# A modulation's weights moved in the load queue, its second half summed in two bursts, and high parts of rows used first, in a two-layer Hyena and attention block

## The chip, the core and the metric

The kernel runs on one core of a Trainium2 chip. A core has TensorE (PE, matrix products), VectorE (DVE), ScalarE (ACT), GpSimd (POOL) and SyncE (SP, which here issues loads and stores). Each engine runs its own instructions in order and waits on semaphores for the others. The metric is the device time of one execution in microseconds. TensorE's clock is granted at one of two levels, 1.2 and 2.4 GHz; the profile shows which.

## The reference

A block of two layers works on 512 latent tokens and 256 context tokens of width 1024, all in float32. What matters here is the start of layer 0, a Hyena layer:

```
sh, sc, gt = split(silu(c) @ ada_w[0] + ada_b[0], 3)        # modulation, for c and for c_ctx
h  = rms_norm(x, norm_g[0]) * (1 + sc) + sh                  # 512 latent and 256 context rows
proj = h @ w_in                                              # 1024 -> 4 * 2048
filter: h = sin(freq * (z @ w1 + b1)); sin(.. w2 ..); sin(.. w3 ..); h @ w4, times a decay
x0, x1, v = short convolutions of proj;  u = x1 * v
y = (circular convolution of u with the filter + u * d) * x0 * silu(z),  then @ w_out
```

Layer 1 is attention with grouped heads; the change does not touch it.

## The kernel before

A float32 product is made from three matmuls on rounded parts: an operand is split into a high part (a cast to a 32-bit format with fewer bits) and a low part (the operand minus its high part), and high times high, high times low and low times high are added in PSUM. So every weight tile and every row of h needs a cast and a subtraction. Rows here are the eight blocks of 128 channels of h (k = 0 to 7); each has 512 latent and 256 context columns: `h_hi`, `h_lo` and `hc_hi`, `hc_lo`.

The program is written in one order per engine by hand: up to the first u (L685) every instruction of an engine follows the one written before it (the class `Engine`, L58, whose call is L69, so that nearly all rows of the first 70 us carry line L69). Behind that a scheduler orders the work.

How the start runs:

- SP loads x and the context (12 halves), then the weights of the modulation's shift and scale. These stand in two halves of the output channels, each as eight tiles of 512 KB (`ada0_load(dh, k)`, L344; tiles 2 to 7 of the first half as two loads). Between them stand the first two weight tiles of the projection (`st16`, `st32`: the tiles for x1 and v, L426) and the filter's last weights (`w4s0`). Eight loads are in flight at most: each waits for the one eight places ahead.
- TensorE multiplies the modulation's tiles as they come (`ada0`, L372, into `prow`); ScalarE copies the sums (`srow`), eight small matmuls turn them into columns (`padc`), and VectorE adds the bias and makes `ada` and `gsc` (`ada0_cols`, L380). The first half serves rows 0 to 3, the second rows 4 to 7.
- `load_w` (L125) splits a weight tile: the cast on ScalarE, the subtraction on GpSimd. `first_w` holds the tiles of the two outputs 16 and 32 (the second called `fw`) and of 17.
- `begin` (L595) interleaves rows and projections. `write(k)` calls `h_write` (L229): ScalarE scales and shifts (`raw` for rows 0 to 3, `hf` for 4 to 7), VectorE casts and subtracts, GpSimd subtracts for the context. `step(e, k)` is six matmuls of output e with row k (`in_step`, L580, into `pl` and `pc`).
- The third layer of the filter's small network (`mlp_mm(2)`, L283, then `mlp_arg`, a range reduction on VectorE, `mlp_sin`, `mlp_end` into `h3`) and the first group of the filter (`kfilter`, L475: `w4h`, `w4l`, then six `lags`, each two matmuls `pk` and a product `kfl` or `kfc`) are written among these.
- After `begin`, GpSimd issues four loads (kmat, kfwd) and starts `kdft` (L527): sums and differences `F0m`, their cast on ScalarE (`Fh0m`) and the low part (`Fl0m`), and so on, for the filter's transform; TensorE goes on with projections and later with the transform of u (`pu`).

The changed places are `h_write`, `mlp_end`, `ada0_cols`, the loads at L422 to L433, the first weights at L463 to L470, and `begin`.

Of the kernel before, what the change touches and what calls it, by code (L numbers as in the profile page):

```python
# [52 lines left out]
def hybrid_kernel(ctx: ExitStack, tc: tile.TileContext, x, ctxt, cols, fws, ada_w, hy_w_in, fw4, hy_w_out, at_w_in, at_q_g, at_k_g, at_w_out,  # L53
# [38 lines left out]
    def f(ap):  # L92
        return ap.bitcast(F32)
# [85 lines left out]
    def axt(name):  # L179
        return pa.tile([P, 512], F32, tag="ax", name=name, bufs=4)  # L180
# [48 lines left out]
    def h_write(k, src):  # L229

        t = raw.get(k)
        if t is None:
            t = cvtile(f"hf{k}")
        for s, hi, lo, c_, en in ((0, h_hi, h_lo, slice(0, LL), V), (1, hc_hi, hc_lo, slice(LL, T), G)):
            S.activation(t[:, c_], src(s), AF.Identity, bias=col_sh(0, s, k), scale=col_gsc(0, s, k))
            V.tensor_copy(hi[:, k, :], t[:, c_])
            r = en.tensor_tensor(lo[:, k, :], t[:, c_], f(hi[:, k, :]), ALU.subtract)
        hc_done.append(r)

# [14 lines left out]
    def cvtile(name):  # L254
        return hp.tile([P, T], F32, tag="cv", name=name, bufs=5)
# [58 lines left out]
    def mlp_sin(hh=0):  # L314
        aa = feat[0][:, hh * 384:hh * 384 + 384]
        S.activation(aa, aa, AF.Sin)

    def mlp_end():
        a = feat[0]
        if "h3" in dbg:  # L320
            SY.dma_start(dbg["h3"], a)
        h3t = hp.tile([P, T], F32R, tag="sz", name="h3t")
        V.tensor_copy(h3t, a)
        V.tensor_copy(h3[0:64], f(h3t[0:64]))
        V.tensor_tensor(h3[64:128], a[64:128], f(h3t[64:128]), ALU.subtract)
# [18 lines left out]
    def ada0_load(dh, k):  # L344

        c_ = slice(dh * 512, dh * 512 + 512)
        src = ada_w[0][k * P:(k + 1) * P, 0:2 * DM].rearrange("p (x o) -> p x o", x=2)[:, :, c_]
        two = "p (x o) -> p x o"
        if dh == 0 and k < 2:
            t = abtile(f"ad{dh}_{k}").rearrange(two, x=2)  # L350
        elif dh and k < 2:
            if k == 0:
                ad_st["big"] = kg.tile([P, 4, 512], F32, tag="kfl", name=f"ad{dh}_{k}")
            t = ad_st["big"][:, k * 2:k * 2 + 2, :]
        elif dh and k == 2:
# [24 lines left out]
    def ada0_cols(dh):  # L380
        srow = cvtile(f"srow{dh}")
        S.copy(srow[:, 0:512], prow[dh])
        padc = axt(f"padc{dh}")
        for j in range(4):
            TE.matmul(padc[:, j * 4:j * 4 + 4], srow[:, j * P:(j + 1) * P], sel2.rearrange("p x s -> p (x s)"),
                      start=True, stop=True)
        pv = padc[:, 0:16].rearrange("p (j x s) -> p s x j", x=2, s=2)
# [33 lines left out]

    for i in range(12):  # L422
        load_x(i)
    for k in range(6):
        ada0_load(0, k)
    st16, st32 = (wp.tile([P, 1024], F32, tag="stg", name=f"stg{e}", bufs=NST) for e in (16, 32))  # L426
    SY.dma_start(st16.rearrange("p (k e) -> p k e", k=KD), load_first(16))
    ada0_load(0, 6)
    SY.dma_start(st32.rearrange("p (k e) -> p k e", k=KD), load_first(32))
    ada0_load(0, 7)  # L430
    w4s0 = load_w4(0)
    for k in range(KD):
        ada0_load(1, k)  # L433
# [28 lines left out]
            ada0(0, 4 + k // 2)  # L462
    for i in range(1, 12, 2):  # L463
        scale_x(i, i in (3, 7, 11))
    first_w = {16: load_w(None, (KD, P), st=st16)}
    first_w[32] = load_w(None, (KD, P), st=st32, more=lambda i: [
        hp.tile([P, 1024], F32R, tag="AB", name=f"fw{x}", bufs=NAB) for x in range(2)])
    ada0(0, 6)
    ada0(0, 7)
    ada0_cols(0)  # L470


    kfs, kts = {}, {}
# [121 lines left out]
    def begin(es):  # L595

        for e in es:
            begun[e] = mmt(f"pl_{e}"), mmt(f"pc_{e}")
        pts = {}

        def write(k):
            h_write(k, (lambda s: raw[k][:, 0:LL] if s == 0 else raw[k][:, LL:T]) if k in raw else
                    (lambda s: pts[k][s][:, 0:LL if s == 0 else LC]))

        def step(e, k):
            cur[0] = in_step(first_w[e], *begun[e], k)
# [17 lines left out]
        first_w[17] = load_w(load_first(17), (KD, P))
        step(es[1], 3)
        ada0(1, 6)
        ada0(1, 7)
        ada0_cols(1)
# [880 lines left out]
```

## Time and profile before

| | us |
|---|---|
| median of 3 runs | 1477.99 (1475.77 to 1478.94) |
| profiled execution | 1477.03 |
| its span, first to last instruction | 1475.3 |
| TensorE busy in the span | 1433.8 (97%) |
| VectorE, ScalarE, GpSimd busy | 1081.9, 558.6, 488.5 |
| mean granted clock of TensorE | 0.994 of 2.4 GHz |

TensorE is busy 97% of the span, but its first slices are not full: in the page's row of 40 slices (36.9 us each) PE stands at 5 in the first and at 9 after it. GpSimd is busy a third of the whole, but 8.5 and 8.9 of 10 us in 70 to 80 and 80 to 90 us. Busy shares are averages over stages: here the reader has to look at who waits for whom in the first 110 us. A timeline row gives start, duration, engine, line, operation, output and inputs, count, and in brackets the idle time before it and what ended it. A chain row gives start, duration and what the end hung on. A DVE or POOL row that is longer than others of its shape holds a wait that is not shown as idle time.

### The profile page before, as it was taken

To read this page: it belongs to the slowest core of one execution; us is meant where nothing else is said; L and a number is where in the kernel's file an instruction comes from. 1 tells how busy PE (TensorE), PEld (TensorE's weight loads), DVE (VectorE), ACT (ScalarE), POOL (GpSimd) and SP (SyncE) were. 2 spreads that over 40 slices of the span, in tenths; PEclk is the share of its full clock that TensorE was granted. 3 is DMA by queue.
4 is the path that set the end of the run, shared out by engine and by line. 5 is a ranking of instruction groups with operands and counts; after the bars stand their busy time and mean duration, and the time that the engine had idled before them with its cause. 6 is when DMAs were issued, how large, how long until landed. Compare 5 with 4: busy or idle time off the path is not lost.

```text
span 1475.3 us, 23743 instructions
## 1 busy us (share of the span) xinstructions
PE 1433.8 (97%) x9271; PEld 1252.5 (85%) x9271; DVE 1081.9 (73%) x1904; ACT 558.6 (38%) x1089; POOL 488.5 (33%) x437
## 2 busy tenths in 40 slices
PE   5999999999999999999998999999999999999998
PEld 1688888888888888888887888799998998998987
DVE  3869769588695885968858354756886878878886
ACT  5332322323223233232333243634455444444442
POOL 1472735527345264462554451211100000000005
PEclk9999999999999999999999999999999999999999
DMA  9611433324223233232313774255222212212111
GB/s 321 187 52 57 122 87 90 93 76 122 80 82 111 72 115 93 79 108 79 90 55 109 275 274 159 75 166 170 91 90 86 86 44 78 94 44 72 58 61 69
DMA packets 177308, 157.58 MB, mean 107 GB/s; under 512 B 6771, under 2 KB 154891, under 8 KB 176684
## 3 DMA queue, kind: packets, MB, share of 16 engines
q1 hardware_dynamic: 173340, 135.10, 30.0%
q0 software_dynamic: 3712, 20.45, 4.0%
q8 instruction: 73, 1.20, 0.3%
q10 hardware_dynamic: 144, 0.52, 0.1%
q14 instruction: 39, 0.32, 0.1%
HBM read 138.20 MB, written 17.84 MB: 106 GB/s over the span
## 4 chain that ended last, share of the span: by engine, by line
PE 74%; DVE 16%; DMA 4%; POOL 3%; issue 1%; ACT 1%; SPq 1%; POOLq 0%; ACTq 0%; DVEq 0%
PE po L89 3%; PE po L90 3%; PE et L1293 3%; PE po L88 3%; PE pq L771 3%; DVE Y L724 3%; PE plx L582 3%; PE plx L583 2%; PE plx L586 2%; PE px L89 2%; PE px L88 2%; PE px L90 2%; PE pz L88 2%; PE pz L89 2%; PE pz L90 2%; PE pq L88 2%
## 5 line engine op out<-in xcount | busy, mean ns | idle before, releaser
L141 POOL TENSOR_TENSOR wlo<-stg,whi 128x1024 fp32r<-128x1024 f32 x63 | 154.1, 2446 | 202.2 <-ACT whi L140 201.4
L140 ACT CAST whi<-stg 128x1024 fp32r<-128x1024 f32 x97 | 101.8, 1050 | 251.1 <-issue 180.2
L1052 POOL TENSOR_TENSOR r2q<-s2q,mhalf 128x2 f32<-128x2 f32 x32 | 23.5, 733 | 342.1 <-DVE s2q L1050 342.1
L1281 ACT ACTIVATE E<-sc,st 128x768 f32<-128x768 f32 x64 | 57.7, 901 | 128.0 <-DVE st L1279 115.3
L582 PE MATMUL plx<-h_hi,whi 128*128 128x512 f32 x248 | 100.7, 406 | 0.0
L583 PE MATMUL plx<-h_lo,whi 128*128 128x512 f32 x248 | 98.1, 396 | 0.0
L586 PE MATMUL plx<-h_hi,wlo 128*128 128x512 f32 x248 | 98.1, 395 | 0.0
L1278 DVE TENSOR_REDUCE st<-sc 128x1 f32<-128x768 f32 x64 | 61.0, 953 | 16.6 <-PE sc L90 16.3
L585 PE MATMUL pcx<-hc_lo,whi 128*128 128x256 f32 x248 | 69.9, 282 | 0.0
L587 PE MATMUL pcx<-hc_hi,wlo 128*128 128x256 f32 x248 | 69.4, 280 | 0.0
L584 PE MATMUL pcx<-hc_hi,whi 128*128 128x256 f32 x248 | 69.4, 280 | 0.0
L1298 DVE TENSOR_TENSOR ptl<-et,pth 128x768 fp32r<-128x768 f32 x64 | 61.0, 954 | 5.3 <-ACT pth L1297 4.1
L931 DVE TENSOR_TENSOR yl<-yf,yh 128x768 fp32r<-128x768 f32 x26 | 25.8, 995 | 51.4 <-ACT yh L930 51.2
L1297 ACT CAST pth<-et 128x768 fp32r<-128x768 f32 x64 | 51.1, 799 | 31.1 <-PE et L1293 31.0
L585 PEld LDWEIGHTS pcx<-hc_lo,whi 128*128 128x128 f32 x248 | 46.7, 188 | 11.1
L584 PEld LDWEIGHTS pcx<-hc_hi,whi 128*128 128x128 f32 x248 | 46.7, 188 | 11.1
L90 PE MATMUL po<-pth,kvt 128*128 128x256 f32 x192 | 54.2, 283 | 0.0
L582 PEld LDWEIGHTS plx<-h_hi,whi 128*128 128x128 f32 x248 | 46.8, 189 | 8.7 <-issue 0.4
L89 PE MATMUL po<-ptl,kvt 128*128 128x256 f32 x192 | 54.1, 282 | 0.0
L88 PE MATMUL po<-pth,kvt 128*128 128x256 f32 x192 | 54.0, 281 | 0.0
L698 DVE TENSOR_TENSOR utl<-ut,uth 128x512 fp32r<-128x512 f32 (+1 forms) x32 | 16.4, 552 | 49.7 <-ACT uth L697 49.7
L1293 PE MATMUL et<-ident,E 128*128 128x128 f32 x384 | 52.3, 272 | 0.1
(911 smaller groups left out, 5129.0 us busy)
## 6 DMA issues: line engine op xcount, KB each, us to landing
stg<-in_hy_w_in_dram SPq DMA_DIRECT2D x64, 512.0 KB, 4.2
stg<-in_at_w_in_dram SPq DMA_DIRECT2D x40, 512.0 KB, 4.2
adw<-in_ada_w_dram SPq DMA_DIRECT2D x32, 512.0 KB, 3.8
yf<-y_scr POOLq DMA_DIRECT2D x32, 384.0 KB, 5.1
stg<-in_hy_w_out_dram SPq DMA_DIRECT2D x16, 512.0 KB, 5.5
stg<-in_at_w_out_dram SPq DMA_DIRECT2D x16, 512.0 KB, 3.6
dec<-in_k_dec_dram SPq DMA_DIRECT2D x48, 128.0 KB, 2.5
y_scr<-y SPq DMA_DIRECT2D x16, 384.0 KB, 3.2
```

The lines of the kernel that those rows point to most:

```text
L88: TE.matmul(ps, lh, rh, start=first, stop=False)
L89: TE.matmul(ps, lh, rl, start=False, stop=False)
L90: TE.matmul(ps, ll, rh, start=False, stop=last)
L140: S.copy(hi, st)
L141: (lo_eng or lo_default[0] or G).tensor_tensor(lo, st, f(hi), ALU.subtract)
L582: TE.matmul(pl, hi[:, k, :], h_hi[:, k, :], start=fi, stop=False)
L583: TE.matmul(pl, hi[:, k, :], h_lo[:, k, :], start=False, stop=False)
L584: TE.matmul(pc[:, 0:LC], hi[:, k, :], hc_hi[:, k, :], start=fi, stop=False)
L585: TE.matmul(pc[:, 0:LC], hi[:, k, :], hc_lo[:, k, :], start=False, stop=False)
L586: TE.matmul(pl, lo[:, k, :], h_hi[:, k, :], start=False, stop=la)
L587: return TE.matmul(pc[:, 0:LC], lo[:, k, :], hc_hi[:, k, :], start=False, stop=la)
L1293: TE.transpose(tp_[:, b * P:(b + 1) * P], E[:, b * P:(b + 1) * P], ident)
```

## The change

- The queue: all eight tiles of the modulation's first half are loaded ahead of `st16` and `st32`, which stood behind tiles 5 and 6.
- The first half's sums are copied and turned ahead of the split of the first weight tile. For output 32 the cast goes from ScalarE to VectorE (written behind the columns) and the subtraction on GpSimd behind row 0's.
- The second half's eight tiles are used in two bursts of four: after row 2, and while the range reduction runs. They were used in four pairs of two among rows 1 to 3. Copy and turn are separate functions now, `ada0_sum` and `ada0_turn`.
- In `h_write` both high parts of a row are made before the low parts; in `step` the six matmuls go in the order high by high, low weights by high rows, high weights by low rows.
- The third layer's matmuls and the filter's w4 split move from row 1 to row 2. Its `h3` is made by two copies on ScalarE and a subtraction on GpSimd, where VectorE did all three.
- Weight tile 17 is loaded and split ahead of the range reduction (it stood behind it), and each of the six lags stands a place later.

```
         t = raw.get(k)
...
+        parts = (h_hi, h_lo, slice(0, LL), V), (hc_hi, hc_lo, slice(LL, T), G)
+        for s, (hi, lo, c_, en) in enumerate(parts):
             S.activation(t[:, c_], src(s), AF.Identity, bias=col_sh(0, s, k), scale=col_gsc(0, s, k))
             V.tensor_copy(hi[:, k, :], t[:, c_])
+        for hi, lo, c_, en in parts:
             r = en.tensor_tensor(lo[:, k, :], t[:, c_], f(hi[:, k, :]), ALU.subtract)
...
-        V.tensor_copy(h3t, a)
-        V.tensor_copy(h3[0:64], f(h3t[0:64]))
-        V.tensor_tensor(h3[64:128], a[64:128], f(h3t[64:128]), ALU.subtract)
+        S.copy(h3t, a)
+        S.copy(h3[0:64], f(h3t[0:64]))
+        G.tensor_tensor(h3[64:128], a[64:128], f(h3t[64:128]), ALU.subtract)
...
+    def ada0_sum(dh):
+        srow[dh] = cvtile(f"srow{dh}")
+        S.copy(srow[dh][:, 0:512], prow[dh])
+
+    def ada0_turn(dh):
+        padc = padc_[dh] = axt(f"padc{dh}")
...
-    for k in range(6):
+    for k in range(KD):
         ada0_load(0, k)
...
-    ada0_load(0, 6)
     SY.dma_start(st32.rearrange("p (k e) -> p k e", k=KD), load_first(32))
-    ada0_load(0, 7)
...
-    first_w = {16: load_w(None, (KD, P), st=st16)}
-    first_w[32] = load_w(None, (KD, P), st=st32, more=lambda i: [
...
     ada0(0, 6)
     ada0(0, 7)
+    ada0_sum(0)
+    ada0_turn(0)
+    first_w = {16: load_w(None, (KD, P), st=st16)}
     ada0_cols(0)
+    fw32 = [hp.tile([P, 1024], F32R, tag="AB", name=f"fw{x}", bufs=NAB) for x in range(2)]
+    first_w[32] = [t.rearrange("p (a b) -> p a b", a=KD) for t in fw32]
+    V.tensor_copy(fw32[0], st32)
...
         def step(e, k):
-            cur[0] = in_step(first_w[e], *begun[e], k)
+
+            (hi, lo), (pl, pc), fi, la = first_w[e], begun[e], k == 0, k == KD - 1
+            for i, (w, l, c) in enumerate(((hi, h_hi, hc_hi), (lo, h_hi, hc_hi), (hi, h_lo, hc_lo))):
...
             write(i)
+            if i == 0:
+                G.tensor_tensor(fw32[1], st32, f(fw32[0]), ALU.subtract)
             step(es[0], i)
             if i:
                 step(es[1], i - 1)
-
-                ada0(1, 2 * i - 2)
-                ada0(1, 2 * i - 1)
-            if i == 1:
+            if i == 2:
+
+                for k in range(4):
+                    ada0(1, k)
                 mlp_mm(2)
                 lags += kfilter(0, w4s0)
-        for hh in range(2):
-            mlp_arg(2, hh)
-            mlp_sin(hh)
+        first_w[17] = load_w(load_first(17), (KD, P))
+        mlp_arg(2, 0)
+        mlp_sin(0)
+        for k in range(4, 8):
+            ada0(1, k)
+        ada0_sum(1)
+        mlp_arg(2, 1)
+        step(es[1], 3)
+        ada0_turn(1)
+        ada0_cols(1)
+        mlp_sin(1)
         mlp_end()
```

What this does to the order is shown at three places. First SP's queue, behind tile 5 of the modulation's first half (`ad`; `stg` are the projection's first two weight tiles, `hy_w_in`):

```order
-L69 DMA stg_159<-in_hy_w_in_dram 128x8x128
-L69 DMA ad_6_0_162<-in_ada_w_dram 128x512
-L69 DMA ad_6_1_163<-in_ada_w_dram 128x512
-L69 DMA stg_160<-in_hy_w_in_dram 128x8x128
-L69 DMA ad_7_0_167<-in_ada_w_dram 128x512
-L69 DMA ad_7_1_168<-in_ada_w_dram 128x512
+L69 DMA ad_6_0_159<-in_ada_w_dram 128x512
+L69 DMA ad_6_1_160<-in_ada_w_dram 128x512
+L69 DMA ad_7_0_163<-in_ada_w_dram 128x512
+L69 DMA ad_7_1_164<-in_ada_w_dram 128x512
+L69 DMA stg_167<-in_hy_w_in_dram 128x8x128
+L69 DMA stg_168<-in_hy_w_in_dram 128x8x128
```

Tiles 6 and 7 moved ahead of both weight tiles. Second, GpSimd from its first weight tile on, before:

```order
L69 TENSOR_TENSOR wlo_309<-stg_159,whi_308 128x1024
L69 TENSOR_TENSOR fw_313<-stg_160,fw_312 128x1024
L69 TENSOR_TENSOR hc_lo<-raw_254,hc_hi 128x256
L69 TENSOR_TENSOR hc_lo<-raw_265,hc_hi 128x256
L69 TENSOR_TENSOR w4l_376<-w4s_171,w4h_375 128x512
L69 TENSOR_TENSOR hc_lo<-raw_278,hc_hi 128x256
L69 TENSOR_TENSOR hc_lo<-raw_289,hc_hi 128x256
L69 TENSOR_TENSOR wlo_449<-stg_447,whi_448 128x1024
```

Four long pieces (128x512 and more) stand among the context's low parts. And now:

```order
L69 TENSOR_TENSOR wlo_320<-stg_167,whi_319 128x1024
L69 TENSOR_TENSOR hc_lo<-raw_254,hc_hi 128x256
L69 TENSOR_TENSOR fw_328<-stg_168,fw_327 128x1024
L69 TENSOR_TENSOR hc_lo<-raw_265,hc_hi 128x256
L69 TENSOR_TENSOR hc_lo<-raw_278,hc_hi 128x256
L69 TENSOR_TENSOR w4l_398<-w4s_171,w4h_397 128x512
L69 TENSOR_TENSOR hc_lo<-raw_289,hc_hi 128x256
L69 TENSOR_TENSOR wlo_423<-stg_421,whi_422 128x1024
L69 TENSOR_TENSOR h_116<-ma_396,h3t 64x768
```

The low part of fw stands between rows 0 and 1, w4l a row later, and the subtraction for h3 (`h`) is new on this engine. VectorE has the cast of fw (`fw_327`) between the columns and row 0. Third, ScalarE behind row 3, before (`ma` is the argument of the filter's last sine, `whi_448` weight tile 17):

```order
L69 ACTIVATE raw_289<-raw_289,ada_83,gsc_85 128x256
L69 ACTIVATE ma_374<-ma_374 128x384 x2
L69 CAST whi_448<-stg_447 128x1024
L69 COPY srow_463<-prow_365 128x512
L69 ACTIVATE hf_490<-xT_0_474,ada_83,gsc_85 128x512
```

Both sines stand ahead of the weight tile's cast. And now:

```order
L69 ACTIVATE raw_289<-raw_289,ada_83,gsc_85 128x256
L69 CAST whi_422<-stg_421 128x1024
L69 ACTIVATE ma_396<-ma_396 128x384
L69 COPY srow_444<-prow_383 128x512
L69 ACTIVATE ma_396<-ma_396 128x384
L69 CAST h3t<-ma_396 128x768
L69 CAST h_116<-h3t 64x768
L69 ACTIVATE hf_490<-xT_0_474,ada_83,gsc_85 128x512
```

The cast of weight tile 17 moved ahead of the sines, and the two copies for h3 came from VectorE.

## Rows read from the trace of the kernel before

**Rows 1.** Chain of waits, 13 to 38 us: start us, duration us, what.

```profile
20.44 2.45 SPq L69
...
22.93 6.79 DMA ad<-in_ada_w_dram
...
34.26 0.18 DVE ada L69
...
35.56 0.44 DVE h_hi L69
```

**Rows 2.** Timeline of TensorE, 24 to 55 us.

```profile
24.67 2.13 PE L69 MATMUL prow<-ad,silp 128*32 128x512 f32 x8
28.29 1.05 PE L69 MATMUL prow<-ad,silp 128*32 128x512 f32 x2 [1.49 <-DMA ad<-in_ada_w_dram]
29.77 1.90 PE L69 MATMUL prow<-ad,silp 128*32 128x512 f32 x2 [0.43 <-DMA ad<-in_ada_w_dram]
...
53.24 1.05 PE L69 MATMUL padc<-sel,srow 128*128 128x4 f32 x8 [0.84 <-ACT srow L69]
```

**Rows 3.** Windows: busy us (instructions) by engine, granted clock, DMA share, GB/s.

```profile
26.00:28.00 2.00, 0.80 (x3) 0.00 (x0) 0.39 (x1) 2.00 (x4) 0.00 (x1) 1.00 1.11 339
28.00:30.00 2.00, 1.28 (x3) 0.31 (x4) 0.00 (x0) 0.87 (x1) 2.00 (x1) 0.95 1.10 217
40.00:42.00 2.00, 2.00 (x14) 1.41 (x17) 1.97 (x4) 0.13 (x1) 1.76 (x2) 0.99 1.15 325
56.00:58.00 2.00, 1.38 (x5) 0.68 (x5) 1.28 (x5) 1.94 (x4) 0.00 (x0) 1.00 0.84 240
108.00:112.00 4.00, 3.66 (x15) 3.37 (x16) 1.84 (x3) 0.60 (x2) 1.82 (x1) 0.57 0.15 39
```

**Rows 4.** Chain of waits, 38 to 70 us.

```profile
43.61 0.67 DVE ma L69
...
50.82 0.53 ACT ma L69
...
56.06 0.79 ACT hf L69
```

**Rows 5.** Timeline of GpSimd, 69 to 75 us.

```profile
69.30 0.78 POOL L544 TENSOR_TENSOR F0m<-kfl 128x256 f32<-128x256 f32 x1
...
73.70 1.30 POOL L551 TENSOR_TENSOR Fl0m<-F0m,Fh0m 128x512 fp32r<-128x512 f32 x1 [0.58 <-ACT Fh0m L550]
```

**Rows 6.** Timeline of TensorE, 104 to 109 us.

```profile
107.61 0.38 PE L88 MATMUL pu<-uth,kfwd 128*128 128x256 f32 x1 [1.77 <-ACT uth L697]
```

**Rows 7.** Timeline of GpSimd, 28 to 55 us.

```profile
28.00 2.35 POOL L69 TENSOR_TENSOR wlo<-stg,whi 128x1024 fp32r<-128x1024 f32 x1 [9.23 <-ACT whi L69]
...
39.49 1.73 POOL L69 TENSOR_TENSOR w4l<-w4s,w4h 128x512 fp32r<-128x512 f32 x1
...
43.13 0.73 POOL L69 TENSOR_TENSOR hc_lo<-raw,hc_hi 128x256 fp32r<-128x256 f32 x1 [0.83 <-DVE hc_hi L69]
52.36 2.37 POOL L69 TENSOR_TENSOR wlo<-stg,whi 128x1024 fp32r<-128x1024 f32 x1 [8.49 <-ACT whi L69]
```

**Rows 8.** Timeline of VectorE, 36 to 56 us.

```profile
36.63 0.28 DVE L69 CAST hc_hi<-raw 128x256 fp32r<-128x256 f32 x1
...
40.00 1.38 DVE L69 CAST hc_hi<-raw 128x256 fp32r<-128x256 f32 x1
...
51.38 0.56 DVE L69 CAST h3t<-ma 128x768 fp32r<-128x768 f32 x1 [0.59 <-ACT ma L69]
...
52.54 3.01 DVE L69 TENSOR_TENSOR h<-ma,h3t 64x768 fp32r<-64x768 f32 x1
```

**Rows 9.** Timeline of ScalarE, 67 to 74 us.

```profile
67.50 1.05 ACT L140 CAST whi<-stg 128x1024 fp32r<-128x1024 f32 x1 [2.22 <-PE pc L69]
...
73.01 0.61 ACT L550 CAST Fh0m<-F0m 128x512 fp32r<-128x512 f32 x1
```

**Rows 10.** Waits, 0 to 80 us: who for whom, us in total, times, longest.

```profile
PE pc L69 <- POOL hc_lo L69: 0.8, 2, 0.4
```

More of the change, by code (lines that the diff above doesn't have):

```diff
@@ L233, in h_write @@
             t = cvtile(f"hf{k}")
-        for s, hi, lo, c_, en in ((0, h_hi, h_lo, slice(0, LL), V), (1, hc_hi, hc_lo, slice(LL, T), G)):
+        parts = (h_hi, h_lo, slice(0, LL), V), (hc_hi, hc_lo, slice(LL, T), G)
+        for s, (hi, lo, c_, en) in enumerate(parts):
             S.activation(t[:, c_], src(s), AF.Identity, bias=col_sh(0, s, k), scale=col_gsc(0, s, k))
             V.tensor_copy(hi[:, k, :], t[:, c_])
+        for hi, lo, c_, en in parts:
             r = en.tensor_tensor(lo[:, k, :], t[:, c_], f(hi[:, k, :]), ALU.subtract)
@@ L378, in ada0 @@
             TE.matmul(prow[dh][q:q + 32, :], silp[:, 2 * k:2 * k + 32], t, start=k < 2, stop=k >= KD - 2)
-    def ada0_cols(dh):
[L381 to L387, printed above, removed]
+    srow, padc_ = {}, {}
+    def ada0_sum(dh):
[3 more added lines that the diff above has]
+        padc = padc_[dh] = axt(f"padc{dh}")
+        for j in range(4):
+            TE.matmul(padc[:, j * 4:j * 4 + 4], srow[dh][:, j * P:(j + 1) * P], sel2.rearrange("p x s -> p (x s)"),
+                      start=True, stop=True)
+    def ada0_cols(dh):
+        pv = padc_[dh][:, 0:16].rearrange("p (j x s) -> p s x j", x=2, s=2)
         bv = vb[:, 32:48].rearrange("p (x k) -> p x k", x=2)[:, :, dh * 4:dh * 4 + 4]
@@ L464, in hybrid_kernel @@
         scale_x(i, i in (3, 7, 11))
-    first_w = {16: load_w(None, (KD, P), st=st16)}
-    first_w[32] = load_w(None, (KD, P), st=st32, more=lambda i: [
-        hp.tile([P, 1024], F32R, tag="AB", name=f"fw{x}", bufs=NAB) for x in range(2)])
     ada0(0, 6)
     ada0(0, 7)
+    ada0_sum(0)
+    ada0_turn(0)
+    first_w = {16: load_w(None, (KD, P), st=st16)}
     ada0_cols(0)
+    fw32 = [hp.tile([P, 1024], F32R, tag="AB", name=f"fw{x}", bufs=NAB) for x in range(2)]
+    first_w[32] = [t.rearrange("p (a b) -> p a b", a=KD) for t in fw32]
+    V.tensor_copy(fw32[0], st32)
     kfs, kts = {}, {}
@@ L605, in step @@
         def step(e, k):
-            cur[0] = in_step(first_w[e], *begun[e], k)
+            (hi, lo), (pl, pc), fi, la = first_w[e], begun[e], k == 0, k == KD - 1
+            for i, (w, l, c) in enumerate(((hi, h_hi, hc_hi), (lo, h_hi, hc_hi), (hi, h_lo, hc_lo))):
+                TE.matmul(pl, w[:, k, :], l[:, k, :], start=fi and i == 0, stop=la and i == 2)
+                cur[0] = TE.matmul(pc[:, 0:LC], w[:, k, :], c[:, k, :], start=fi and i == 0, stop=la and i == 2)
         lags = []
@@ L613, in begin @@
                 step(es[1], i - 1)
-                ada0(1, 2 * i - 2)
-                ada0(1, 2 * i - 1)
-            if i == 1:
+            if i == 2:
+                for k in range(4):
+                    ada0(1, k)
                 mlp_mm(2)
                 lags += kfilter(0, w4s0)
-        for hh in range(2):
-            mlp_arg(2, hh)
-            mlp_sin(hh)
-        mlp_end()
[L624 to L628, printed above, removed]
+        first_w[17] = load_w(load_first(17), (KD, P))
[9 more added lines that the diff above has]
+        mlp_sin(1)
+        mlp_end()
         for k in (4, 5):
@@ L632, in begin @@
             write(k)
-            lags.pop(0)()
+            if k > 4:
+                lags.pop(0)()
             if k in (5, 6):
@@ L638, in begin @@
                 step(es[1], 4)
-        for _ in range(2):
+        for _ in range(3):
             lags.pop(0)()
```

## The prediction

> **What bounds the kernel now.** The page first: the span is 1475.3 us and the profiled execution took 1477.03, so 1.7 us lie around the span, and it is 0.96 us below the median of the runs shown (1477.99). I make the sum on this execution and carry the difference to the median. Everything that the change moves stands before 74 us; behind that each engine runs the same instructions in the same order, so the question is by how much one hand-over point moves. I read the chain of waits over the first 70 us, then each engine's timeline there, then the windows for the granted clock, then the place near 106 us where TensorE waits again.
>
> In the chain the reader is to see a queue: the last tile of the modulation's first half lands at 29.72 (22.93 + 6.79), and the scale and shift columns (ada) are written at 34.26 [rows 1]. TensorE uses the tiles that it has until 26.8, waits 1.49 and 0.43 us for the last two and sums these at half clock [rows 2]: the granted clock is 0.95 in 28 to 30 and 0.99 in 40 to 42, so it fell to 1.2 of 2.4 GHz at 29.9 and rose at 40.0 [rows 3]. Then rows 0 to 3 are converted, VectorE does the range reduction of the filter's last sine until 50.8, and ScalarE begins rows 4 to 7 at 56.06 [rows 4]. The hand-over point is GpSimd's F0m at 69.30 [rows 5]: from there GpSimd works with few pauses until TensorE's pu, which waits 1.77 us and starts at 107.61 [rows 6]. So GpSimd's chain decides what a gain before 69.30 is worth, and it hands it on whole.
>
> **The change part by part.**
>
> *Queue.* Tiles 6 and 7 no longer stand behind 1.05 MB of projection weights. At the 339 GB/s of that stretch [rows 3] this is 3.1 us; and one issue that took 2.45 us [rows 1] was held up in the same queue. So the last tile lands at 26.6, or at 25.2 if half of that issue is won too. TensorE takes 2.13 us for the pairs of two tiles from 24.67 [rows 2], about 0.5 us a tile if none is missing; the sums are ready at 26.7 to 27.6 instead of 31.67. I take 26.7, since the tiles come faster than they are used. ScalarE copies the sums (0.6, at 27.6 with what stands ahead of it), eight small matmuls take 1.05 at full clock [rows 2]: ada at 28.7 instead of 34.26. If these 5.6 us stayed, the kernel would be 5 us faster. What is late next?
>
> *Weights after the turn.* ScalarE casts whi at 27.6 to 28.6 and GpSimd makes wlo at 28.6 to 30.9 (2.35, [rows 7]). Both stood under the wait for the modulation's weights, which covered them; now they stand beside the columns. (Weight tile 16 lands 1.6 us behind the last tile, 26.8 to 28.2: at the late end all of this moves by 0.6.) The high part of the second weight tile, fw, moves from ScalarE to VectorE, ahead of all row conversions. It could start at 29.3, after four small operations, and there GpSimd's wlo is running. What happens then the trace shows: the cast hc_hi takes 0.28 us alone, and 1.38 at 40.00, ending 0.16 after GpSimd's w4l (39.49 + 1.73); h takes 3.01 from 52.54 and ends 0.8 after wlo (52.36 + 2.37) [rows 7, 8]. So VectorE's cast waits until 30.9 and ends at 31.5 (0.70 by itself: 0.28 for 256 columns, 0.56 for 768, [rows 8]). Behind it wait the conversions of rows 0 to 3, and behind them TensorE's first projection step and GpSimd's hc_lo. Row 0's h_hi is ready at 32.0 instead of 36.0 [rows 1]: 4.0 of 5.6 us are left.
>
> The Trainium skill ("SBUF — State Buffer", Who interferes with whom) states it as a rule, and it speaks against this order: VectorE and GpSimd share a port pair as an exclusive lock, and whichever starts later is blocked for the whole instruction. By it the cast can't pass wlo, and the two long rows agree.
>
> *Rows 0 to 3.* Per row VectorE needs some 1.25 us (casts of 512 and 256 columns, 0.42 and 0.28, and a subtraction, about 0.55) and GpSimd 0.59 (0.73 less its start), which can't overlap: 7.4 for four rows. Between them GpSimd now makes the low part of fw, as long as wlo, which was under the wait before, and w4l: 2.2 and 1.2 without their starts [rows 7]. 10.8 us from 31.5: the last hc_lo ends at 42 instead of 43.86 (43.13 + 0.73). 1.9 us are left. Using high parts first helps TensorE only where it waits for low parts; here it is late for nothing else.
>
> *Bursts.* The matmuls of the filter's third layer stood behind two tiles of the modulation's second half, and now behind four tiles and a later row. From row 2 at 40.0: its step until 40.8, the other weight tile's 1.1, four tiles at 0.5, and 0.85: VectorE can begin the range reduction at 44.9 instead of 43.61 [rows 4]. It takes 7.2 us (43.61 to 50.8). GpSimd's wlo of weight tile 17 stood behind it, at 52.36 [rows 7]; now, with its load landing at 43.4 as before and its cast, it falls at 44.6 to 46.9, beside it. The first operation reads PSUM and I let it pass, the second waits: 1.2 us. The arguments are ready at 53.3 instead of 50.8.
>
> *After it.* Before: the sine, three operations on VectorE (0.56, 0.55, 3.01) and four small ones, 5.2 us from 50.82 to 56.06 [rows 4, 8]. Now the columns are ready beside it, and ScalarE does both copies of 768 columns, 0.83 each (between 0.61 for 512 and 1.05 for 1024, [rows 9]). The subtraction goes to GpSimd: about 1.8 us, until 56.6, covered, since the first pk stands behind a step and comes at 58.5. Sine and copies are 2.1: rows 4 to 7 begin at 55.4, **0.65 earlier**.
>
> *Rows 4 to 7.* F0m came 13.2 us after their start. TensorE waits here for low parts, 0.8 us for hc_lo alone [rows 10]; high parts first gives back about half: **0.45**. Against it, TensorE has little between 52.9 and 57.0, some 3 us empty and one small piece. Before, with work spread over 52 to 58, the clock stayed at 1.00 [rows 3]; but it fell after 1.49 + 0.43 us of waiting at 29.9, and after the 1.77 us at 107.6 it was 0.57 over 108 to 112, so at half for 3.4 us [rows 2, 3, 6]. If it falls here, the matmuls of rows 4 to 7 lose about 1.1 on their chain. I count it as even: 0.55.
>
> *Behind F0m.* ScalarE's cast Fh0m stood behind two activations that wait for TensorE, and GpSimd waited 0.58 for it [rows 5, 9]. It now stands ahead of them: **0.58**. Edits at nothing: the filter products (lags) stand a place later, covered by some 3 us before F0m reads them; the second half's loads, dec and kinv keep their places in SP's queue, and the buffers that they wait for there become free sooner.
>
> Sum: 0.65 + 0.45 + 0.58 = 1.7 without the fall of the clock, 0.6 with it; the middle, **1.2 us faster**: 1475.8 on this execution's scale, 1476.8 on the median's. What no row prices: weight tile 17 may land 0.8 sooner (0.8 more gained); the lock in the range reduction may cost nothing or the whole 2.4, that is 1.2 either way.
>
> **Rivals.**
> 1. *The lock doesn't bite* (the cast gets in before wlo, and GpSimd's pieces fall into VectorE's pauses). For it: 5.6 us are there to be had. Against it: the two rows where they met, and four long GpSimd instructions in the way. Then F0m comes 4.4 to 5 us earlier: 1473.
> 2. *The wait at 106 shrinks so far that the clock holds.* 0.58 of the gain shortens GpSimd's chain but not TensorE's work ahead of pu, so of 1.77 us 1.2 remain. If the clock then holds, half of 3.4 us goes too: 1.7 + 1.7 = 3.4, 1474.6. Against it: it fell after such a wait at 29.9.
> 3. *Slower: the clock stays low.* Place: TensorE from 30 on, its first step at 32 and then waits for row 1, and again from 57. If the clock comes back at 47 instead of 40, the third layer is 3.1 us later, the arguments are ready at 55.3 and rows 4 to 7 begin 1.25 late; a fall for twice as long there costs 2.6. 1.25 + 2.6 - 0.45 - 0.58: 2.8 slower, 1480.8. It decides if the steps after 36 are too thin to bring the clock back. Against it: steps as dense brought it back at 40.
>
> **How the numbers follow.** Forecast 0.62, rival 1 0.08, rival 2 0.15, rival 3 0.15. About 0.2% (3.0 us) is what a measurement of this kernel can tell from no change. Faster by more (below 1475.0): rival 1, nearly all of rival 2, and the forecast's edge with the earlier load, 0.25. Slower by more (above 1480.9): half of rival 3, 0.08. Within: 0.67. The range leaves out rival 1 and the far half of rival 3: 1473.6 to 1480.3.
>
> **What would show it.** The sums' end near 26.7 and ada near 28.7 (queue); VectorE's cast of fw near 2.3 us long and ending with wlo (lock); row 3's hc_lo near 42; the second operation of the range reduction over 1 us; the first hf near 55.4; the granted clock in 57 to 61; F0m at 68 to 69; Fl0m without a wait. I am wrong if the cast is short, if F0m moves by more than 2.5 us, or if what stands behind 74 us gives the gain back.

## The result and the profile after

| | before | after |
|---|---|---|
| median of 4 runs, us | 1476.88 (1475.66 to 1478.94) | 1485.43 (1484.99 to 1485.63) |
| profiled execution | 1477.03 | 1485.63 |
| its span | 1475.3 | 1483.9 |
| mean granted clock | 0.994 | 0.988 |

The changed kernel is slower: 1.0058 times the time before, 95% interval 1.0046 to 1.0070, some 8.5 us. The forecast was 1.2 us faster. All of the loss arises ahead of 84 us; behind that the same instructions come 8.6 to 8.9 us later, to the end. The points that the prediction named, in us from the start of the span:

| point | before | predicted | after |
|---|---|---|---|
| last sum of the modulation's first half ends | 31.67 | 26.7 | 26.41 |
| row 0's h_hi ready | 35.99 | 32.0 | 32.04 |
| last hc_lo of rows 0 to 3 ends | 43.86 | 42 | 41.91 |
| range reduction starts | 43.59 | 44.9 | 44.62 |
| its arguments are ready | 50.79 | 53.3 | 53.87 |
| first hf of row 4 | 56.06 | 55.4 | 56.06 |
| F0m | 69.30 | 68 to 69 | 70.74 |
| plx, the next projection | 71.77 | (1.2 earlier) | 78.02 |
| pu | 107.61 | (1.2 earlier) | 116.40 |

Down to the range reduction the prediction holds within 0.3 us. Then three things go wrong, and the largest was in no term of the sum. The chain of waits, 69 to 79 us (start, duration, what the end hung on), shows it:

```profile
68.89 0.48 PE pk L69 x2
69.39 0.70 DVE kfl L69
70.11 5.53 DMA dec<-in_k_dec_dram
75.74 0.69 DVE kfc L69
76.43 0.67 DVE cvx L69
77.12 0.76 DVE cvx L69
77.88 0.14 issue
78.02 0.77 PE plx L591
```

Read it upwards. TensorE's next projection needs the PSUM bank that VectorE's convolution (cvx) empties; that stands behind the last product of the filter, kfc; that waits for a load of 128 KB, dec, the filter's decay, which took 5.5 us from issue to landing (VectorE stands idle for 3.5 of them). The load was issued at 70.11 only, since it goes into one of two buffers and waits until the fourth lag's product (kfl) has read it. In the kernel before neither kfc nor plx had a wait (VectorE, then TensorE):

```profile
69.49 0.69 DVE L69 TENSOR_TENSOR kfc<-pk,dec 128x512 f32<-128x512 f32 x1
```

```profile
71.77 0.47 PE L582 MATMUL plx<-h_hi,whi 128*128 128x512 f32 x1
```

TensorE's timeline of the changed kernel, with the rows that answer [rows 2, 6] (idle time ahead of a row and its cause in brackets):

```profile
24.50 1.91 PE L69 MATMUL prow<-ad,silp 128*32 128x512 f32 x12
27.34 1.05 PE L69 MATMUL padc<-sel,srow 128*128 128x4 f32 x8 [0.93 <-ACT srow L69]
...
51.41 1.05 PE L69 MATMUL padc<-sel,srow 128*128 128x4 f32 x8 [1.41 <-ACT srow L69]
...
57.58 0.80 PE L69 MATMUL pl<-h_hi,whi 128*128 128x512 f32 x1 [2.55 <-DVE h_hi L69]
...
78.02 0.77 PE L591 MATMUL plx<-h_hi,whi 128*128 128x512 f32 x1 [4.55 <-DVE cvx L69]
...
116.40 0.39 PE L88 MATMUL pu<-uth,kfwd 128*128 128x256 f32 x1 [1.78 <-ACT uth L716]
```

The windows of the same kernel (length, busy us by PE, PEld, DVE, ACT and POOL with instructions, granted clock, DMA share, GB/s), which answer [rows 3]:

```profile
52.00:54.00 2.00, 2.00 (x15) 1.72 (x14) 1.86 (x6) 0.10 (x1) 0.00 (x0) 0.74 0.61 144
56.00:58.00 2.00, 0.42 (x1) 0.42 (x2) 1.14 (x3) 2.00 (x5) 1.38 (x2) 0.50 0.00 0
60.00:62.00 2.00, 2.00 (x9) 1.70 (x8) 0.69 (x2) 0.33 (x1) 0.60 (x1) 0.50 0.00 0
62.00:64.00 2.00, 2.00 (x9) 1.72 (x9) 1.32 (x3) 0.90 (x2) 0.69 (x1) 0.70 0.22 66
...
72.00:74.00 2.00, 1.47 (x9) 1.01 (x7) 0.20 (x1) 1.18 (x2) 2.00 (x2) 1.00 1.12 380
74.00:76.00 2.00, 0.00 (x0) 0.00 (x0) 0.26 (x1) 0.67 (x2) 1.92 (x3) 1.00 0.79 252
76.00:78.00 2.00, 0.00 (x0) 0.01 (x1) 1.97 (x4) 0.62 (x1) 1.27 (x3) 0.71 0.17 50
80.00:82.00 2.00, 2.00 (x10) 1.81 (x8) 1.93 (x4) 0.00 (x0) 1.08 (x3) 0.50 0.17 49
82.00:84.00 2.00, 2.00 (x8) 1.72 (x8) 1.97 (x4) 0.00 (x0) 0.00 (x0) 0.58 0.00 0
```

The clock falls twice more than before, to 1.2 GHz: from 53 to 63, behind TensorE's wait of 1.41 us for the copy of the sums, and from 77 to 84, inside the wait for plx. At 74 to 76 TensorE does nothing at all while the DMA engines are busy 0.79 of the time. The 8.79 us at pu add up from the two traces: the last projection step ahead of plx ends 1.57 later (73.47 against 71.90), plx stands 4.55 behind it where it stood at once (4.68 more), and the last 2.54 are lost behind plx, while the clock is at half.

The other engines: VectorE's and GpSimd's rows that answer [rows 5, 7, 8].

```profile
28.64 2.03 DVE L69 SCALAR_TENSOR_TENSOR gsc<-ada,vb 128x4 f32<-128x4 f32 x1
30.86 0.69 DVE L69 CAST fw<-stg 128x1024 fp32r<-128x1024 f32 x1
46.12 3.81 DVE L69 SCALAR_TENSOR_TENSOR ma<-mn,ma 128x384 f32<-128x384 f32 x3
75.74 0.69 DVE L69 TENSOR_TENSOR kfc<-pk,dec 128x512 f32<-128x512 f32 x1 [3.54 <-DMA dec<-in_k_dec_dram]
```

```profile
28.31 2.34 POOL L69 TENSOR_TENSOR wlo<-stg,whi 128x1024 fp32r<-128x1024 f32 x1 [9.83 <-ACT whi L69]
45.79 2.54 POOL L69 TENSOR_TENSOR wlo<-stg,whi 128x1024 fp32r<-128x1024 f32 x1 [3.89 <-ACT whi L69]
70.74 0.78 POOL L553 TENSOR_TENSOR F0m<-kfl 128x256 f32<-128x256 f32 x1
74.44 1.29 POOL L560 TENSOR_TENSOR Fl0m<-F0m,Fh0m 128x512 fp32r<-128x512 f32 x1
```

A gsc of 128x4, 0.16 us alone, took 2.03 and ended at 30.67, with GpSimd's wlo (30.65). The three operations at 46.12, 1.75 in the second half of the range reduction, took 3.81 beside the other wlo.

### The profile page after: what moved, and what is told of

The parts are those of the page before. It is cut to its first block, busy times and chain, and to the rows that moved or that the text cites. A ratio compares the mean times of both kernels' runs of the same rounds, so it can differ in the third digit from the quotient of the medians.

```text
span 1483.9 us, 23743 instructions
## 1 busy us (share of the span) xinstructions
PE 1435.3 (97%) x9271; PEld 1257.3 (85%) x9271; DVE 1083.9 (73%) x1902; ACT 559.2 (38%) x1090; POOL 492.8 (33%) x438
## 4 chain that ended last, share of the span: by engine, by line
PE 77%; DVE 15%; POOL 2%; DMA 2%; issue 2%; ACT 1%; SPq 0%; POOLq 0%; ACTq 0%; DVEq 0%
PE po L90 4%; PE po L89 4%; PE po L88 4%; PE pq L790 3%; PE et L1312 3%; DVE Y L743 3%; PE plx L591 3%; PE plx L592 2%; PE plx L595 2%; PE px L89 2%; PE px L88 2%; PE px L90 2%; PE pz L88 2%; PE pz L90 2%; PE pz L89 2%; PE pq L88 2%
## 5 line engine op out<-in xcount | busy, mean ns | idle before, releaser
L594 PEld LDWEIGHTS pcx<-hc_lo,whi 128*128 128x128 f32 x248 | 47.1, 190 | 11.3
L593 PEld LDWEIGHTS pcx<-hc_hi,whi 128*128 128x128 f32 x248 | 47.1, 190 | 11.2
```

Of the source, the lines that this page charges most:

```text
L593: TE.matmul(pc[:, 0:LC], hi[:, k, :], hc_hi[:, k, :], start=fi, stop=False)
L594: TE.matmul(pc[:, 0:LC], hi[:, k, :], hc_lo[:, k, :], start=False, stop=False)
```

## The experiments

Times are medians of 9 to 11 runs where no other number stands, ratios are to the kernel before on the same chip. That kernel had 1476.74 beside experiments 1 to 4, 1477.00 beside 5 to 8 and 1477.12 beside 9 to 12, and each ratio is known to about 1.4 us either way, so a difference of 1 us between two experiments is not clear of the noise. Identical instructions ahead of 27 us already lie up to 1.5 us apart between two executions, so single times of two traces are compared only over stretches.

**1. The lags back in their old places.** Is the late load the cause, or only a consequence of the clock's fall at 53?

```
-            if k > 4:
-                lags.pop(0)()
+            lags.pop(0)()
...
-        for _ in range(3):
+        for _ in range(2):
             lags.pop(0)()
```

> The changed kernel with one part undone: the six lags of the filter's first group stand at their old places, one place earlier. Theory L (the load): the last dec tile's load waits for the product of the fourth lag (two buffers), which now comes at 69.4, so it is issued at 70.11, behind the four loads of kmat and kfwd, and lands at 75.65; the last kfc, the convolution behind it on VectorE and with it the PSUM bank of the next projection wait, TensorE idles 4.55 us before plx and its clock falls for 6.8 us behind that. By L the lags' old places issue that load near 68.5, it lands near 71, plx starts at 73.3 without a wait and the clock holds: 1485.4 - 7.3 = 1478.1 (1477.5 to 1478.7). Rival C (the clock): all of the loss starts with the fall of the clock at 53 us, which makes rows 4 to 7 late, and the late load is only its consequence; then the kernel stays at 1483 or more.

Measured: 1478.45, ratio 1.0012 (1.0003 to 1.0022). The clock fell near 55 all the same, and yet 7.0 of the 8.5 us are gone: theory L holds, C falls. Both waits are short now, though not nothing as expected (VectorE and TensorE):

```profile
71.58 0.69 DVE L69 TENSOR_TENSOR kfc<-pk,dec 128x512 f32<-128x512 f32 x1 [0.54 <-DMA dec<-in_k_dec_dram]
...
73.86 0.47 PE L591 MATMUL plx<-h_hi,whi 128*128 128x512 f32 x1 [0.31 <-DVE cvx L69]
```

**2. The later places kept, the load early.** The last two dec tiles go into unused columns of the small network's weight tile.

```
+        for tl in (4, 5):
+            pre[tl] = fwt[:, (tl - 3) * 256:(tl - 2) * 256]
+            nc.sync.dma_start(pre[tl], k_dec[tl][:, 0:256])
...
+            dc = pre.pop(tl, None) if g == 0 else None
+            if dc is None:
+                dc = k0.tile([P, 256], F32, tag="dec", name=f"dec{g}_{tl}", bufs=2)
```

> The changed kernel with the lags at their new, later places, but the dec tiles of lags 4 and 5 loaded into columns of the small network's weight tile that nobody uses, at 37 us, without a wait for a buffer. Theory L: the load alone was the cause, so the same 1478.1 (1477.5 to 1478.7) and no wait for dec. If the later place of the lags on TensorE and VectorE itself were the cause (rival O, the order): 1485 as before this edit. Rival C: 1483 or more.

Measured: 1479.09, ratio 1.0018 (1.0009 to 1.0027), 0.4 above the expected range; 6.3 us come back without a change of order. plx starts at 73.62 with no wait. The later places themselves cost little at most (0.6 above experiment 1, within the noise); their loads cost the rest.

**3. The same part alone, on the kernel before.**

```
             write(k)
-            lags.pop(0)()
+            if k > 4:
+                lags.pop(0)()
...
-        for _ in range(2):
+        for _ in range(3):
             lags.pop(0)()
```

> The kernel before with this one part of the change: each lag one place later. Theory L: the fourth lag's product comes at about 68.5, the last dec load is issued near 69 behind kmat and kfwd (66.95 to 69.3), lands near 74.6; plx starts near 77 instead of 71.77 and the clock falls for some 6 to 7 us: 1476.9 + 5.2 + 2.5 = 1484.6 (1482 to 1486). Rival C: the clock does not fall at 53 here, so nothing is late: 1476.9 within 0.5.

Measured: 1486.24 in 4 runs, ratio 1.0067 (1.0050 to 1.0084), 0.2 above the expected range. The one part by itself loses as much as the whole change. The trace is of the fastest of the four executions (1483.2). VectorE and TensorE there:

```profile
73.77 0.69 DVE L69 TENSOR_TENSOR kfc<-pk,dec 128x512 f32<-128x512 f32 x1 [4.48 <-DMA dec<-in_k_dec_dram]
...
76.05 0.76 PE L582 MATMUL plx<-h_hi,whi 128*128 128x512 f32 x1 [4.79 <-DVE cvx L69]
```

What makes the load slow is seen in the DMA issues of the last dec load (KB, us from issue to landing), taken from short windows: of the changed kernel (issued at 70.11),

```profile
dec<-in_k_dec_dram SPq DMA_DIRECT2D x1, 128.0 KB, 5.5
```

of experiment 3 (67.93),

```profile
dec<-in_k_dec_dram SPq DMA_DIRECT2D x1, 128.0 KB, 5.8
```

of the kernel before (66.84, 0.1 us ahead of GpSimd's issue of kmat),

```profile
dec<-in_k_dec_dram SPq DMA_DIRECT2D x1, 128.0 KB, 2.6
```

and of experiment 1 (69.07, beside kmat's first load).

```profile
kmat<-in_k_khi_dram POOLq DMA_DIRECT2D x1, 512.0 KB, 4.3
dec<-in_k_dec_dram SPq DMA_DIRECT2D x1, 128.0 KB, 2.4
```

GpSimd issues kmat and kfwd, 1.5 MB, as soon as the last hc_lo is done (in the changed kernel 68.40 to 70.74). Its first issue before, and then now:

```profile
66.95 0.76 POOL L69 DMA_DIRECT2D kmat<-in_k_khi_dram  x1
```

```profile
68.40 0.76 POOL L69 DMA_DIRECT2D kmat<-in_k_khi_dram  x1
```

A dec load that is issued 0.1 us ahead of the first or behind it took 2.4 to 2.9 us in eight traces; the two that were issued 1.7 and 2.1 us behind the first, beside the fourth, took 5.5 and 5.8. So the load is late twice: it is issued 3.3 us later (66.84 to 70.11), of which 1.5 are rows 4 to 7 being late (kmat itself moves from 66.95 to 68.40) and 1.8 the place, and it takes 3 longer.

**4. Matmuls without use, to hold the clock** (on the kernel of experiment 1).

```
         step(es[1], 3)
...
+        for _ in range(6):
+            TE.matmul(padc_[1][:, 32:512], first_w[32][0][:, 3, :], h_hi[:, 3, 0:480], start=True, stop=True)
...
+        for _ in range(3):
+            for s, pt in enumerate(pts[5]):
+                for t in range(4 if s == 0 else 2):
+                    TE.transpose(pt[:, t * P:(t + 1) * P], halves[(t + 4 * s) * 2 + 1][:, P:2 * P], ident)
```

> The lags at their old places, and matmuls without use on TensorE in the two empty stretches of the changed kernel at 50.0 to 51.4 and 55.0 to 57.4 (six 128x480 into unused columns of padc, and row 5's transposes three times more). It asks what the fall of the clock at 53 us costs by itself. If the clock then holds from 53 to 63, F0m comes near 69.2 instead of 70.7: 1476.6, that is 1.5 below the same kernel without them. If the clock falls all the same, or if the chain of rows 4 to 7 doesn't hang on TensorE's speed: no difference to that kernel, 1478.1, or up to 0.5 above it for the matmuls themselves.

Measured: 1479.02, ratio 1.0014 (1.0004 to 1.0023): no gain. The clock held from 42 to 110:

```profile
54.00:56.00 2.00, 1.40 (x13) 1.16 (x12) 1.86 (x7) 0.30 (x1) 0.00 (x0) 1.00 0.44 105
58.00:60.00 2.00, 1.43 (x9) 1.06 (x8) 1.34 (x3) 2.00 (x4) 1.37 (x2) 1.00 0.00 0
```

and from the first hf to the last hc_lo it took 10.3 us, not 11.5 as in experiment 1 and 12.4 in the changed kernel. But kmat came sooner with it, still 0.1 us ahead of the dec load, which took 2.9 us, and the last kfc waited again, 1.04 us (VectorE):

```profile
71.22 0.69 DVE L69 TENSOR_TENSOR kfc<-pk,dec 128x512 f32<-128x512 f32 x1 [1.04 <-DMA dec<-in_k_dec_dram]
```

From the third layer's end to plx 0.7 of the 1.2 us are left in the trace (27.1 against 27.8), and none in the medians.

**5. The third layer ahead of the burst** (on experiment 1).

```
+                mlp_mm(2)
                 for k in range(4):
                     ada0(1, k)
-                mlp_mm(2)
```

> The kernel with the lags at their old places, and the matmuls of the filter's third layer ahead of the burst of four modulation tiles behind row 2 instead of behind it. Theory B (the bursts cost what stands on the chain): the eight matmuls of the burst are 1.92 us on the chain from row 2 to the range reduction, so the arguments, the first hf of row 4 and plx come 1.9 earlier: 1478.45 - 1.9 = 1476.5. From the third layer's end to the first hf it stays at 11.5 us, as in the changed kernel. Rival P: TensorE's own work up to plx is the limit, not the range reduction; then less than 0.5 is gained.

Measured: 1476.97, ratio 0.9998 (0.9988 to 1.0007), 1.5 below experiment 1; the two intervals overlap. The trace bears theory B out: from the last hc_lo of rows 0 to 3 to the third layer's end it takes 1.7 us instead of 3.4, and 11.5 from there to the first hf, as expected. But in this execution the clock also held from 43 to the end of rows 4 to 7, which take 10.3 us instead of 11.5, so the 2.0 us by which plx comes earlier are not the burst's alone.

**6. Weight tile 17's low part on VectorE** (on experiment 1), where VectorE waits for row 4.

```
-        first_w[17] = load_w(load_first(17), (KD, P))
...
+        SY.dma_start(st17.rearrange("p (a b) -> p a b", a=KD), load_first(17))
+        S.copy(w17[0], st17)
...
         ada0_cols(1)
+        V.tensor_tensor(w17[1], st17, f(w17[0]), ALU.subtract)
```

> The kernel with the lags at their old places, and the low part of weight tile 17 made by VectorE behind the modulation's second columns, not by GpSimd during the range reduction. Theory K (the lock): the three SCALAR_TENSOR_TENSOR of the range reduction's first half took 3.81 us instead of 1.75 beside that GpSimd instruction, so 2.06 come back and the third layer's end to the first hf takes 9.4 us instead of 11.5; the copy of the sums is no longer late either, TensorE does not wait 1.41 us for it, and if its clock then holds from 53 to 63 the stretch from the first hf to the last hc_lo takes 10.3 instead of 11.5. 1475.2 to 1476.4. Rival P: TensorE's work is the limit, less than 0.5 gained. If VectorE was slow there for another reason than GpSimd, 11.5 stays.

Measured: 1475.01, ratio 0.9990 (0.9980 to 0.9999), 3.4 below experiment 1, 0.2 below the expected range, and just faster than before. VectorE:

```profile
47.64 1.75 DVE L69 SCALAR_TENSOR_TENSOR ma<-mn,ma 128x384 f32<-128x384 f32 x3
...
53.79 1.23 DVE L69 TENSOR_TENSOR wlo<-stg,whi 128x1024 fp32r<-128x1024 f32 x1
```

The 2.06 us are back and the clock held from 42 on: theory K. In this execution, and in that of experiment 5, it also held behind the wait for pu, after a wait as long as ever (TensorE here, then its window):

```profile
106.71 0.39 PE L88 MATMUL pu<-uth,kfwd 128*128 128x256 f32 x1 [1.76 <-ACT uth L720]
```

```profile
108.00:112.00 4.00, 4.00 (x28) 3.61 (x27) 3.11 (x3) 0.00 (x0) 0.92 (x1) 1.00 0.42 123
```

Against before, pu comes 0.90 earlier and what follows behind 120 us 2.44: the clock that held is worth 1.5.

**7. Both edits together** (5 and 6).

```
+                mlp_mm(2)
                 for k in range(4):
...
+        V.tensor_tensor(w17[1], st17, f(w17[0]), ALU.subtract)
```

> Both edits together: third layer ahead of the burst, weight tile 17's low part on VectorE. If both are on the chain they add: plx 4 to 5 us earlier than with the lags alone put back, 1473.5 to 1474.5, faster than the kernel before (1476.7). Rival P: the transposes of rows 4 and 5 and the second burst stand on TensorE ahead of row 4 and become the limit; then it gains no more than the better of the two alone.

Measured: 1474.27, ratio 0.9981 (0.9972 to 0.9990): 4.2 below experiment 1 and within the expected range. They don't add fully: rows 4 to 7 take 11.2 us here, not 10.3. TensorE and VectorE show what is late next: GpSimd's part of h3, and once more the load.

```profile
55.60 0.50 PE L69 MATMUL pk<-w4h,h 128*128 128x512 f32 x1 [2.16 <-POOL h L69]
...
67.59 0.69 DVE L69 TENSOR_TENSOR kfc<-pk,dec 128x512 f32<-128x512 f32 x1 [0.95 <-DMA dec<-in_k_dec_dram]
```

**8. The old order of parts** (on experiment 4, so at full clock).

```
-            for i, (w, l, c) in enumerate(((hi, h_hi, hc_hi), (lo, h_hi, hc_hi), (hi, h_lo, hc_lo))):
...
+            cur[0] = in_step(first_w[e], *begun[e], k)
...
             V.tensor_copy(hi[:, k, :], t[:, c_])
-        for hi, lo, c_, en in parts:
             r = en.tensor_tensor(lo[:, k, :], t[:, c_], f(hi[:, k, :]), ALU.subtract)
```

> The kernel with the useless matmuls, in which the clock held from 42 to 110 us, with the old order of parts: high part, low part per half row, and the six matmuls of a step as before. It asks what high parts first is worth by itself, at full clock. By the prediction 0.45 on rows 4 to 7: the stretch from the first hf to the last hc_lo, 10.31 us with high parts first, takes 10.8 to 11.0 (10.96 in the kernel before), and the time is 0.5 longer. If the order is worth nothing, 10.3 and no difference.

Measured: 1480.93, ratio 1.0023 (1.0014 to 1.0033), 1.9 above experiment 4 by the medians, 1.3 by the two ratios. GpSimd's last hc_lo here and ScalarE's first hf:

```profile
69.10 0.73 POOL L69 TENSOR_TENSOR hc_lo<-hf,hc_hi 128x256 fp32r<-128x256 f32 x1 [2.50 <-DVE hc_hi L69]
```

```profile
58.56 1.89 ACT L69 ACTIVATE hf<-xT,ada,gsc 128x512 f32<-128x512 f32 x3
```

From the first hf to the last hc_lo 11.3 us (69.83 - 58.56) against 10.3: high parts first is worth about 1.0 on rows 4 to 7, twice what I took. Only half of it reaches plx (27.7 us behind the third layer's end, against 27.1), since experiment 4 waits there for its load. Another 0.7 stand ahead of the range reduction (46.37 and 47.07), where the clock came back at 43 instead of 42, and 0.6 of the difference between the two traces arise behind 700 us, where both run the same instructions.

**9 and 10. Experiment 7 with the dec loads early, then also with the lags in their later places.** The edit of experiment 2 on the kernel of 7, and behind it that of 1 reversed:

```
+            pre[tl] = fwt[:, (tl - 3) * 256:(tl - 2) * 256]
...
+            if k > 4:
                 lags.pop(0)()
```

> The kernel with the lags at their old places, the third layer ahead of the burst and weight tile 17's low part on VectorE, and now also the last two dec tiles loaded early into unused columns. In the kernel without this edit the last kfc still waited 0.95 us for its dec load and plx 0.68 us for the convolution behind it. Theory L: plx comes 0.7 earlier, 1474.27 - 0.7 = 1473.6. If another operation is as late as the load: no difference.

> The same with the lags at their new, later places, as the change has them. Theory L says that the later places cost nothing once the load is out of the way, and here they could gain: with the lags at the old places TensorE waits 2.16 us for GpSimd's part of h3 ahead of row 4's first step, since the first pk stands in front of it. 0.5 to 0.9 earlier than with the old places: 1472.9 (1472.5 to 1473.6). If the later places cost something by themselves: 1474 or more.

Measured: 1474.23 (ratio 0.9977, 0.9968 to 0.9986) and 1474.22 (0.9981, 0.9972 to 0.9990). Neither differs from experiment 7; both expectations of a gain were wrong, and with the load out of the way the two places of the lags cost the same. In the second kernel plx comes at 69.43, where it came at 69.87 in experiment 7, so there is little to see.

**11. Weight tile 16's low part on VectorE too** (on experiment 10).

```
-    first_w = {16: load_w(None, (KD, P), st=st16)}
...
+    S.copy(w16[0], st16)
     ada0_cols(0)
+    V.tensor_tensor(w16[1], st16, f(w16[0]), ALU.subtract)
...
-    V.tensor_copy(fw32[0], st32)
...
+                S.copy(fw32[0], st32)
                 G.tensor_tensor(fw32[1], st32, f(fw32[0]), ALU.subtract)
```

> The kernel with the dec tiles loaded early and the lags at their later places, and the low part of weight tile 16 on VectorE behind the first columns instead of on GpSimd beside them, the cast of the second weight tile on ScalarE behind row 0. Theory K (the lock): in the changed kernel the first gsc took 2.03 us instead of 0.16 beside GpSimd's low part of tile 16, which ended with it at 30.65; without it the columns end at 29.1, VectorE needs about 1.4 for the low part of tile 16, row 0's h_hi ends near 30.9 instead of 32.04: 1.1 earlier, 1471.8 (1471.2 to 1472.8). If row 0 waits for something else, or the second low part on GpSimd blocks rows 1 and 2 longer instead: no difference.

Measured: 1473.31, ratio 0.9977 (0.9968 to 0.9987). gsc is short again, 0.16 us (VectorE):

```profile
28.90 0.16 DVE L69 SCALAR_TENSOR_TENSOR gsc<-ada,vb 128x4 f32<-128x4 f32 x1
29.25 1.23 DVE L69 TENSOR_TENSOR wlo<-stg,whi 128x1024 fp32r<-128x1024 f32 x1
30.39 0.42 DVE L69 CAST h_hi<-raw 128x512 fp32r<-128x512 f32 x1
```

0.9 below experiment 10 where 1.1 was expected, and outside the expected range, which was reckoned from a 1472.9 that did not come; the intervals of the two overlap. This is the lowest median of the study: by its ratio 3.4 us under the kernel before (1.9 to 4.7), which experiment 9 matches, and some 12 under the changed one.

**12. The load queue alone, on the kernel before.**

```
-    for k in range(6):
+    for k in range(KD):
         ada0_load(0, k)
...
-    ada0_load(0, 6)
...
-    ada0_load(0, 7)
```

> The kernel before with the load queue of the change alone: tiles 6 and 7 of the modulation's first half ahead of the projection's first two weight tiles; all instructions of the engines in their old order. It asks what the queue is worth without the rest. The casts of both weight tiles stand ahead of the copy of the sums on ScalarE, and the second lands at 29.07, so the copy comes at 30.1 instead of 31.7 and ada near 31.9 instead of 34.26; the columns' gsc may then wait for GpSimd's low part of the second weight tile (30.2 to 32.5). Row 0 then 2.0 earlier and all behind it: 1477.0 - 2.0 = 1475.0 (1474.4 to 1476.0). If the lock and the clock (which falls by the end of the sums either way) take it back: 1476.5 to 1477.5.

Measured: 1477.44, ratio 1.0004 (0.9995 to 1.0013): nothing. The columns come 1.4 us earlier (32.85 against 34.26), behind both casts on ScalarE as expected, and so do rows 0 to 3. But behind row 0's first matmul TensorE has no wait until the third layer, and the clock stayed low until 41.0, not 40.0: 6.4 us of that stretch at half clock instead of 4.0, as the window of 40 to 42 (0.75, where [rows 3] has 0.99) shows:

```profile
40.00:42.00 2.00, 2.00 (x14) 1.10 (x12) 1.59 (x3) 0.00 (x0) 1.14 (x2) 0.75 1.17 309
```

The third layer is only 0.35 earlier, and plx as much. Here the clock took back what the queue gave.

## Why the prediction was wrong, step by step

- **Queue, weights after the turn, rows 0 to 3**: right in size (26.41, 32.04 and 41.91 for 26.7, 32.0 and 42). The lock bit where I had not looked: not the cast of fw, but the gsc ahead of it. The sum came out since either ends with wlo. By the rule of the Trainium skill ("SBUF — State Buffer", Who interferes with whom) the later of two instructions on the shared ports waits out the whole of the other; this trace agrees, 30.67 against 30.65.
- **Bursts**: the third layer as predicted (44.62 for 44.9; the terms given add to 44.75). The lock in the range reduction was bounded at 0 to 2.4 and taken at 1.2; it cost 2.06 (3.81 - 1.75), so the arguments came at 53.87 for 53.3. Experiments 5 and 6 price the two at 1.5 and 3.4, each with the clock that held in rows 4 to 7.
- **After it**: 2.15 us from the sine to hf, as predicted (2.1); all of the 0.65 went to the lock.
- **Rows 4 to 7**: two sizes off. High parts first is worth about 1.0, not 0.45 (experiment 8). The clock did fall, for 10 us, and against 10.3 at full clock (experiments 4 to 6) rows 4 to 7 took 12.4: 2.1, where I counted half of 1.1. In experiment 1 it fell for 6.8 us, and they took 11.5. I had seen the idle stretch and priced it by too short a fall.
- **Behind F0m**: Fl0m has no wait, as predicted; F0m to Fl0m is 0.7 shorter. It is worth nothing, since the step "GpSimd's chain decides what a gain before 69.30 is worth" is wrong. In experiment 7 F0m comes 2.4 and Fl0m 2.7 earlier than before, plx 1.90, and pu 1.89: pu follows plx. In the eleven traces with full clock between the two, pu comes 35.7 to 35.9 us behind plx, while F0m to pu varies from 38.2 to 38.9. The hand-over point was TensorE's own plx at 71.77, which had no wait before and so no row in a table of waits.
- **The step that failed** is an edit at nothing: the lags "stand a place later, covered by some 3 us before F0m reads them", while "the buffers that they wait for there become free sooner". The first held (the third lag's product, which F0m reads, ended 2.3 us ahead of it, at 68.45), but it looks only at who reads the product. The second is false: a dec buffer is freed by a lag's product, so a lag one place later frees it later (70.08 instead of 66.80), and the load goes out among 1.5 MB of kmat and kfwd, 1.7 us behind the first of them. In the kernel before this load was issued 0.1 us ahead of them and landed at 69.4, just in time for its product at 69.49. The cover that I named was not the one that counted. This cost 7.0 of 8.5 us (experiment 1); without it the sum was off by 1.7 - (-1.2) = 2.9. In that experiment's trace plx is 3.2 off: 0.9 by the lock, some 0.5 by rows 4 to 7, 0.65 behind F0m, and 1.15 since the third layer ended at 46.05, with a clock that came back at 41.6.
- **Rivals**: 1 did not come. 2 had the price nearly right (1.7 for 1.5, experiment 6) and the condition wrong: the wait did not shrink. 3, the clock, named one of its places, TensorE from 57 on, and 2.6 us for 2.1. The first place (30 to 47) was wrong: the clock was back by 40 in the changed kernel and at 41 to 43 in experiments 1 and 4 to 8. No rival held the load.

## What to carry to other kernels

When a consumer is moved, move its buffer's next load with it in the accounting: ask what the freed buffer lets in, and which bulk loads then stand ahead of it in the DMA engines. A transfer that arrives just in time has no row in a table of waits, so look for loads and PSUM banks that end within some tenths of a microsecond of their use before calling an edit free. Long GpSimd subtractions beside VectorE's chain are better put on VectorE itself, in a stretch where it waits: 1.2 us there against 2.1 of standstill here.

## What the runs showed of the hardware

- A load of 128 KB took 2.4 to 2.9 us from issue to landing ahead of or beside the first of four GpSimd loads (1.5 MB together; eight traces), and 5.5 and 5.8 beside the fourth (the changed kernel and experiment 3).
- In the changed kernel VectorE's gsc of 128x4 took 2.03 us beside a GpSimd subtraction, while ada, which reads PSUM, passed in 0.17 beside the same one.
- Behind the wait for pu, 1.74 to 1.83 us in thirteen traces compared, the clock fell in eleven and held in those of experiments 5 and 6 (1.83 and 1.76). The length of the wait does not tell them apart, and no run settled what does. It need not be the edit: of ten executions each, three of experiment 5 and six of experiment 6 have a mean granted clock of 0.995, the traced ones among them, and the others 0.992 to 0.994. It is worth 1.5 us.
